# The end of a one-core transformer block: last term's weights gated on GpSimd, last row in two halves

## The chip, the cores and the metric

The kernel runs on one core of a Trainium2 chip. The time is device microseconds of one execution, as the median over several; the profile is of one further execution, recorded by the hardware profiler. Engines are named as in the profile: PE does matmuls (PEld is its weight load), DVE is the vector engine, ACT the scalar engine, POOL is GpSimd, SP issues most DMAs.

## The reference, cut to what matters

One layer of a hybrid block over x of 1024 rows by 1024 columns, all in float32: an adaptive RMSNorm, a projection, a state-space mixer and chunked attention side by side, an output projection, then a feed-forward part and a final norm. Only the last lines matter here:

```python
    x = x + g_m * (concat[y_s, y_a] @ w_out)
    h = rmsnorm(x, norm_ffn_w) * (1 + sc_f) + sh_f
    x = x + g_f * ((silu(g) * val) @ w_down)     # [g, val] = causal_dwconv(h @ w_up)
return rmsnorm(x, final_norm_w)
```

`g_f`, the gate, is one factor for each of the 1024 columns, the same for all rows. Gating the product `(...) @ w_down` is therefore the same as gating the columns of `w_down` ahead of the product.

## The kernel before, in words

A float32 matmul is made of three matmuls in a faster format: each operand is split into a high part (a rounding copy, on ACT, L93) and a low part (source minus high part, on DVE, L94), and `mm3` (L83 to L86) adds high·high, high·low and low·high. In the final product the operand that streams (`a`, a slice of `w_down`) has 512 columns, and the one that is loaded as weights (`b`, a slice of the hidden state) 128 rows of x at a time. `wsplit` (L1231) puts both parts into one of five ring buffers named `w`.

The down projection is not computed as one product but, by a Strassen-like scheme, as seven products of halves, in the order P1, Q5, Q6, Q7, Q4, P3, P2. Each runs over 11 slices `k` of 128 hidden channels, taken in six pairs `m` (the sixth has one slice), and over four row blocks `st`: 11·4·3 = 132 matmuls of 512 columns. The slices come from DRAM through 14 slots `s0` to `s13` (`load`, L1473). For P3 the weights are the sum of two slices (`add`, L1566, on DVE); P2 takes `w_down` as it is.

The result has eight row blocks of 128 and two column halves. The right halves (columns 512 to 1023) and rows 4 to 7 are complete before the end. For each of them DVE multiplies by the gate `gf` (L1616), loads and adds the residual (L1619, L1620), ACT sums the squares (L1630), and for right halves POOL multiplies by the final norm's weight (L1634). The left half of rows 0 to 3 is the sum of P1 and P2. P1's part (`p1`) is gated and has the residual already; P2 is the last product.

Who runs when is set by a scheduler at build time; each engine then executes its list in order and waits on semaphores. The last part of P2, its pairs 4 and 5 (three slices), is written out by hand (L1712 to L1725) with `InOrder`, which keeps V, A and T in the written order: for each row block nine matmuls, then on DVE the product times the gate (L1719) and the sum with `p1` (L1720), on ACT the squares, on DVE the sum of the two halves' squares, on POOL the power −1/2 (L1130), and then `out_row`: the right half scaled on ACT, the left half on DVE, and two stores on SP. `out_row` of a row stands behind the sums of the next one. In the profile these hand-ordered instructions all carry line L66.

Of the kernel before, what the change touches and what calls it, by code (L numbers as in the profile page):

```python
# [12 lines left out]
AF = mybir.ActivationFunctionType  # L13
ALU = mybir.AluOpType
PSUM = bass.MemoryType.PSUM

P = 128
# [23 lines left out]
KH = NF // 2  # L41
# [31 lines left out]
def tile_block(ctx: ExitStack, tc: tile.TileContext, x, ccol, pk, w_ada, w_first, w_ft, w_z,  # L73
               w_out, w_up, w_down, bias, fnw, out, dbg=None):
    nc = tc.nc
    V, A, T = (InOrder(tc, e) for e in (nc.vector, nc.scalar, nc.tensor))
    G = nc.gpsimd
# [5 lines left out]
    def mm3(ps, lh, ll, rh, rl, start, stop, more=False):  # L83
        T.matmul(ps, lh, rh, start=start, stop=False, skip_group_check=more)  # L84
        T.matmul(ps, lh, rl, start=False, stop=False, skip_group_check=more)  # L85
        T.matmul(ps, ll, rh, start=False, stop=stop, skip_group_check=more)  # L86
# [28 lines left out]
    def stat(n=1):  # L115
        if stc[0] + n > 64:
            stc[0] = 0
        a = st1[:, stc[0]:stc[0] + n]
        stc[0] += n
        return a  # L120
# [18 lines left out]
    def raw_tile(n=1024):  # L139
        rawc[0] += 1  # L140
        return raws[:, rawc[0] % 2, 0:n]
# [227 lines left out]
    for j in range(2):  # L369
        k = slice(4 * j, 4 * j + 4)  # L370
# [48 lines left out]
    for hh in range(2):  # L419
# [12 lines left out]
        tail = range(split_at, KT)  # L432
        for kt in range(KT):
            if hh == 0:
# [7 lines left out]
                t = raw_tile(768)  # L442
# [21 lines left out]
            if hh == 0:  # L464
                for st in range(4, NT):
# [3 lines left out]
                    if XM[st - 4] == kt:  # L469
                        e = A if st < 6 else V  # L470
# [173 lines left out]
    def gemm_part(p, which, hhs):  # L644
        if which == 0:
            new_pair(p)
        if which == 2 and hhs == H1:
            wh, wl = held.pop(p)
        elif p == 2 and which < 2:
            with tc.issue_after(wpin[0].ins), tc.issue_after(wpin[1].ins):  # L650
                wh, wl = wu_pair(w_ft[8 + 3 * (p - 2) + which], A, V)
        else:
            wh, wl = wu_pair(w_ft[8 + 3 * (p - 2) + which], A, G)
        if which == 2 and hhs == H0:
            held[p] = wh, wl
        outs = {hh: psv.tile([P, 512], F32, tag="acc", bufs=1, name="acc") for hh in hhs}
        gemm_ft(wh, wl, outs, GPIN.get((p, which, hhs), {}), hhs)
        for hh in hhs:
            tmp = tps = None
            if which == 2:  # L660
                tmp, tps = p_tile()[:, 0:512], tp_tile()
            evac_qkv(p, which, hh, outs[hh], tmp, tps)
# [15 lines left out]
    part = lambda *a: (lambda: gemm_part(*a))  # L678
# [78 lines left out]
    halves = [slice(0, 512), slice(512, 1024)]  # L757
# [241 lines left out]
    def ssd_y(c, xdt, xdd, cb, ms_):  # L999
        cs = slice(c * P, (c + 1) * P)  # L1000
        prev, cur = state[c % 2], state[(c + 1) % 2]
        ydp = ssd_tile("ydp")
        for h in range(8):
            pe(T.matmul, ydp[:, h * 64:h * 64 + 64], ms_[h // 4][:, h % 4, :],
               xdt[:, h * 64:h * 64 + 64], start=True, stop=True)
        y = sp.tile([P, 512], F32, tag="yy", bufs=2, name="yy")
        with tc.issue_after(powd[0]) if c == 1 else ExitStack():
            i = G.tensor_tensor(h8(y), h8(xs[:, c, :]), hb("p", c), ALU.mult)
        if c < 2:
            z_fine(c, i.ins)  # L1010
        t = sp.tile([P, 512], F32, tag="yt", bufs=2, name="yt")
        if c > 0:
            yop = ssd_tile("yop")
            for g in range(2):
                pe(T.matmul, yop[:, g * 256:g * 256 + 256], ct_[g][:, cs], prev[:, g * 256:g * 256 + 256],
                   start=True, stop=True)
        if c < NT - 1:
            stp = ssd_tile("stp")
            for g in range(2):
                pe(T.matmul, stp[:, g * 256:g * 256 + 256], cb[:, 2 + g, :],  # L1020
                   xdd[:, g * 256:g * 256 + 256], start=True, stop=True)
            if c > 0:
                with tc.issue_after(powd[0]) if c == 1 else ExitStack():
                    G.tensor_tensor(h8(cur), h8(prev), hb("cd", c), ALU.mult)
                V.tensor_tensor(cur, stp, cur, ALU.add)
            else:
                A.activation(cur, stp, AF.Copy)
        V.tensor_tensor(y, ydp, y, ALU.add)
        if c > 0:
            V.tensor_tensor(h8(t), h8(yop), hb("ea", c), ALU.mult)  # L1030
            V.tensor_tensor(y, y, t, ALU.add)
        return y, t
# [17 lines left out]
    NM = (KH + 1) // 2  # L1050

    def kn(m):
        return min(2, KH - 2 * m)

    gd = {}
    for m in range(NM):
        for n, names in (("x", ("b11",)), ("y", ("t1", "t3")), ("z", ("t2", "t4", "b21", "b22"))):
            t = gd[n, m] = dram.tile([kn(m), P, len(names), 512], F32, name=f"g{n}{m}")
# [68 lines left out]
    def rstd2(m):  # L1127
        ms, r = stat(), stat()
        V.scalar_tensor_tensor(ms, m[0], EPS, m[1], op0=ALU.add, op1=ALU.add)
        G.tensor_tensor(r, ms, mhalf[:, 0:1], ALU.pow)  # L1130
        return r
# [4 lines left out]
    for c in range(NT):  # L1136
        if c == 1:
            ssd_turn(*turn)
        y, t = ssd_y(c, *pre)
# [10 lines left out]
        n, k = ((0, slice(0, 3)), (2, slice(0, 4)), (3, slice(0, 3)))[c] if c < 3 else (c + 1, slice(0, 3))  # L1150
# [196 lines left out]
    for sts in ((0, 1), (2, 3)):  # L1347
        h_raw(sts)
        c = slice(sts[0] * P, sts[-1] * P + P)
# [23 lines left out]
    row = lambda u, o: (lambda: u.sums((o,)))  # L1373
# [7 lines left out]
    c = slice(384, 512)  # L1381
# [43 lines left out]
    lo = [u.prep("Q7", "Q4", True) for u in units]  # L1425
# [79 lines left out]
    def take(n, m):  # L1505
        t = res.pop((n, m))
        for slot in [k for k in busy if busy[k] == (n, m)]:
            del busy[slot]
        return t
# [38 lines left out]
    R4 = range(4)  # L1548
    sub = ALU.subtract

    gf, fnr = (t[:, 0:2, :].rearrange("p a b -> p (a b)") for t in (ya, xs))
# [12 lines left out]
    def add(o, a, b):  # L1564
        with tc.issue_after(los[max(0, len(los) - 3)]):
            V.tensor_tensor(o, a, b, ALU.add)  # L1566
        return o
# [3 lines left out]
    def operands(p, m):  # L1571
        a11, a21, a22 = (res[n, m] for n in ("a11", "a21", "a22"))
        b = take(BN[p], m)
        if p == "Q5":
            add(a11, a11, a21)
            add(a21, a21, a22)
        elif p == "Q6":
            add(a21, a11, a22)
        elif p in ("P3", "P2"):
            a = take("a12" + p, m)  # L1580
            if p == "P3":
                add(a, a, a21)
            return a, b
        return dict(P1=a11, Q5=a21, Q6=a21, Q7=a11, Q4=a22)[p], b

# [3 lines left out]
        pump()  # L1589
        return ab  # L1590

    def step(ps, ab, k, sts):
        a, b = (t[:, :, k % 2, :] for t in ab)
        for st in sts:
            c = slice(st * P, (st + 1) * P)
            mm3(ps[st], b[:, 0, c], b[:, 1, c], a[:, 0, :], a[:, 1, :], k == 0, k == KH - 1)

    def product(p, ps, ready=(), tail=False, between=None):
        last = []
        for m in RM:  # L1600
            ab = ready[m] if m < len(ready) else split_pair(p, m)
            if between:
                between(m)
            for k in range(2 * m, 2 * m + kn(m)):
                if tail and m >= NM - 2:
                    last.append((ab, k))
                else:
                    step(ps, ab, k, R4)
        return last

    def xt_():
# [10 lines left out]
    jc, sq = [0], {}  # L1622

    def junk_():
        jc[0] += 1
        return junk[jc[0] % 6]

    def square(row, dh, src):
        sq[row, dh] = stat()
        A.activation(junk_(), src, AF.Square, scale=1.0 / 32.0, accum_out=sq[row, dh])  # L1630

    def right_half(row, src):
        square(row, 1, src)
        G.tensor_tensor(src, src, fnr[:, halves[1]], ALU.mult)  # L1634

    def out_row(row, lo, hi, r):
        t = buf(("a11_0", "a11_1", "a11_2", "a11_3", "a22_0", "a22_1", "a22_2", "a22_3")[row])
        A.activation(t[:, halves[1]], hi, AF.Copy, scale=r)
        V.scalar_tensor_tensor(t[:, halves[0]], lo, r, fnr[:, halves[0]], op0=ALU.mult, op1=ALU.mult)
        for dh in (1, 0):  # L1640
            nc.sync.dma_start(out[row * P:(row + 1) * P, halves[dh]], t[:, halves[dh]])

    def final(row, lo, hi):
        square(row, 0, lo)
# [2 lines left out]
    def rows(ts):  # L1647
        return [t[:, 512 * j:512 * j + 512] for t in ts for j in range(2)]
# [22 lines left out]
    p1, u2 = (rows([c_tile(n), c_tile(n)]) for n in "gv")  # L1671
# [14 lines left out]
    u3 = rows([buf("u30"), buf("u31")])  # L1686
# [18 lines left out]
    W = banks("d")  # L1705
    last = product("P2", W, tail=True)
# [5 lines left out]
    for e in (T, V, A):  # L1712
        e.on, e.last = True, None
    ready = []
    for st in R4:
        for ab, k in last:
            step(W, ab, k, (st,))
        e = junk_()
        V.tensor_tensor(e, W[st], gf[:, halves[0]], ALU.mult)  # L1719
        V.tensor_tensor(p1[st], p1[st], e, ALU.add)  # L1720
        square(st, 0, p1[st])
        if ready:
            out_row(*ready.pop())
        ready.append((st, p1[st], u3[st], rstd2((sq[st, 0], sq[st, 1]))))
    out_row(*ready.pop())  # L1725
    T.on = V.on = A.on = False
    es_s.close()
    es_ht.close()
# [52 lines left out]
```

## Time and profile before

| What | Value |
|---|---|
| time, median of 3 runs (lowest, highest) | 1173.13 us (1171.16, 1173.28) |
| the profiled execution's span | 1173.1 us |
| mean granted PE clock | 0.995 of full speed |
| PE busy | 1152.5 us, 98% of the span |
| DVE busy | 908.3 us, 77% |
| ACT busy | 586.0 us, 50% |
| POOL busy | 155.5 us, 13% |

No other time of the profiled execution is on the page than its span, which lies 0.03 us under the median. A row of the timeline gives the start in us, the duration, the engine, the line, the operation, the tiles written and read, the shape, and in brackets how long the engine stood idle before and what ended it. A row with x3 merges three neighbours of one kind; its duration is from the first start to the last end.

### The profile page before, as it was taken

To read this page: it belongs to the slowest core of one execution; us is meant where nothing else is said; L and a number is where in the kernel's file an instruction comes from. 1 tells how busy PE (TensorE), PEld (TensorE's weight loads), DVE (VectorE), ACT (ScalarE), POOL (GpSimd) and SP (SyncE) were. 2 spreads that over 40 slices of the span, in tenths; PEclk is the share of its full clock that TensorE was granted. 3 is DMA by queue.
4 is the path that set the end of the run, shared out by engine and by line. 5 is a ranking of instruction groups with operands and counts; after the bars stand their busy time and mean duration, and the time that the engine had idled before them with its cause. 6 is when DMAs were issued, how large, how long until landed. Compare 5 with 4: busy or idle time off the path is not lost.

```text
span 1173.1 us, 15823 instructions
## 1 busy us (share of the span) xinstructions
PE 1152.5 (98%) x5851; PEld 977.1 (83%) x5851; DVE 908.3 (77%) x1352; ACT 586.0 (50%) x978; POOL 155.5 (13%) x179
## 2 busy tenths in 40 slices
PE   8999999999999999999999999999999999999997
PEld 7888888788889988887788888888888888888885
DVE  6846555588896779569999988898888869666986
ACT  5636555664335576586453444334533445433454
POOL 2103232340000256100000000000000000000621
PEclk8999999999999999999999999999999999999999
DMA  8835333155578622241223322332233378633544
GB/s 308 305 93 147 79 84 81 39 180 173 183 247 284 245 82 81 77 140 36 99 108 135 115 80 92 118 130 77 90 108 117 117 273 300 252 117 126 162 135 153
DMA packets 63741, 169.15 MB, mean 144 GB/s; under 512 B 6880, under 2 KB 7344, under 8 KB 62256
## 3 DMA queue, kind: packets, MB, share of 16 engines
q1 hardware_dynamic: 56320, 143.11, 37.0%
q10 hardware_dynamic: 7344, 25.04, 5.4%
q8 instruction: 46, 0.75, 0.3%
q14 instruction: 31, 0.25, 0.1%
HBM read 125.87 MB, written 32.81 MB: 135 GB/s over the span
## 4 chain that ended last, share of the span: by engine, by line
PE 86%; DVE 8%; ACT 3%; issue 2%; POOL 1%; DMA 0%; SPq 0%; POOLq 0%; ACTq 0%; DVEq 0%
PE wops L885 6%; PE dn L86 5%; PE dn L85 5%; PE dn L84 5%; PE uY L86 5%; PE uY L84 5%; PE uY L85 5%; PE uX L86 3%; PE uZ L84 3%; PE uZ L86 3%; PE uZ L85 3%; PE uX L84 3%; PE uX L85 3%; PE s L84 3%; PE s L86 3%; PE s L85 3%
## 5 line engine op out<-in xcount | busy, mean ns | idle before, releaser
L84 PE MATMUL dn<-w 128*128 128x512 f32 x296 | 107.4, 389 | 0.0
L85 PE MATMUL dn<-w 128*128 128x512 f32 x296 | 107.4, 389 | 0.0
L86 PE MATMUL dn<-w 128*128 128x512 f32 x296 | 99.9, 390 | 0.1
L84 PE MATMUL uY<-tH,w 128*128 128x512 f32 x248 | 96.5, 389 | 0.0
L86 PE MATMUL uY<-tH,w 128*128 128x512 f32 x248 | 96.5, 389 | 0.0
L85 PE MATMUL uY<-tL,w 128*128 128x512 f32 x248 | 96.5, 389 | 0.0
L1634 POOL TENSOR_TENSOR ya<-ya,xs 128x512 f32<-128x512 f32 x4 | 18.2, 4588 | 551.0 <-ACT xs L1630 551.0
L93 ACT ACTIVATE w<-ya 128x1024 fp32r<-128x1024 f32 (+1 forms) x41 | 39.1, 954 | 85.2 <-PE uY L86 75.2
L885 PE MATMUL wops<-hH,yhl 128*128 128x512 f32 x224 | 73.0, 397 | 1.2 <-DVE yhl L94 1.2
L86 PEld LDWEIGHTS dn<-w 128*128 128x128 f32 x296 | 55.4, 188 | 12.1 <-DVE w L94 0.8
L85 PEld LDWEIGHTS dn<-w 128*128 128x128 f32 x296 | 55.6, 188 | 11.6
L84 PEld LDWEIGHTS dn<-w 128*128 128x128 f32 x296 | 55.6, 188 | 11.6
L557 POOL TENSOR_SCALAR p<-p,st 128x640 f32<-128x640 f32 (+4 forms) x64 | 44.2, 699 | 114.8 <-DVE st L556 111.0
L93 ACT ACTIVATE w<-xs 128x1024 fp32r<-128x1024 f32 (+1 forms) x41 | 39.1, 955 | 37.0 <-PE uY L86 31.0
L551 DVE CUSTOM_DVE_ANT_0 p<-s,bias 128x640 f32<-128x640 f32 (+4 forms) x58 | 38.0, 673 | 23.1 <-PE tp L586 9.6
L94 DVE TENSOR_TENSOR pt<-tp,pt 128x512 fp32r<-128x512 f32 (+2 forms) x72 | 41.6, 595 | 17.3 <-ACT pt L93 17.0
L86 PEld LDWEIGHTS uY<-tH,w 128*128 128x128 f32 x248 | 46.6, 188 | 9.7
L85 PEld LDWEIGHTS uY<-tL,w 128*128 128x128 f32 x248 | 46.6, 188 | 9.7
L84 PEld LDWEIGHTS uY<-tH,w 128*128 128x128 f32 x248 | 46.6, 188 | 9.6
L1308 DVE SCALAR_TENSOR_TENSOR a<-cv,pkt,a 128x1023 f32<-128x1023 f32 (+1 forms) x40 | 50.9, 1275 | 0.1
L84 PE MATMUL s<-hH,wh 128*128 128x512 f32 x128 | 50.6, 395 | 0.1
L885 PEld LDWEIGHTS wops<-hH,yhl 128*128 128x128 f32 x224 | 41.9, 188 | 10.2 <-DVE yhl L94 2.0
(507 smaller groups left out, 3397.2 us busy)
## 6 DMA issues: line engine op xcount, KB each, us to landing
xs<-in_w_ada_dram SPq DMA_DIRECT2D x20, 512.0 KB, 4.6
gz<-a ACTq DMA_DIRECT2D x10, 1024.0 KB, 5.1
ya<-in_w_up_dram SPq DMA_DIRECT2D x11, 768.0 KB, 4.4
xs<-in_w_up_dram SPq DMA_DIRECT2D x11, 768.0 KB, 4.2
adat<-in_w_ada_dram SPq DMA_DIRECT2D x16, 512.0 KB, 7.1
raws<-in_w_ft_dram SPq DMA_DIRECT2D x15, 512.0 KB, 3.9
qk<-qk SPq DMA_DIRECT2D x56, 128.0 KB, 2.3
wos<-in_w_ada_dram SPq DMA_DIRECT2D x12, 512.0 KB, 4.6
```

The costliest lines, as they stand in the source:

```text
L84: T.matmul(ps, lh, rh, start=start, stop=False, skip_group_check=more)
L85: T.matmul(ps, lh, rl, start=False, stop=False, skip_group_check=more)
L86: T.matmul(ps, ll, rh, start=False, stop=stop, skip_group_check=more)
L93: i = A.activation(hi, src, AF.Copy) if ehi is A else ehi.tensor_copy(hi, src)
L94: return i, elo.tensor_tensor(lo, src, f32(hi), ALU.subtract)
L551: V.tensor_tensor_reduce(out=dst, in0=src, in1=bsl, scale=-1.0, scalar=3e38, op0=ALU.add, op1=ALU.min, accum_out=nm)
L557: last_g.append(G.tensor_scalar(pv_, pv_, rr, 1.0, op0=ALU.mult, op1=ALU.mult).ins)
L885: i = op(*a, **k)
L1308: V.scalar_tensor_tensor(a[:, j:S], c[:, 0:S - j], w[2 - j], a[:, j:S], op0=ALU.mult, op1=ALU.add)
L1634: G.tensor_tensor(src, src, fnr[:, halves[1]], ALU.mult)
```

## The change

Three edits. First, in `operands`, P2's slice of `w_down` is multiplied in place by the left half of the gate on POOL, between its load and its split: five multiplies of 128x1024 and one of 128x512. In the last stage DVE's multiply by the gate goes away; DVE adds the product straight from PSUM to `p1`. Second, the last row block's nine tail matmuls of 512 columns become two sets of nine with 256 columns; after each set DVE adds that half and ACT sums its squares, and a further small DVE addition joins the first half's sum of squares to the right half's. Third, of the last row's two stores the right half is issued on ACT's queue; the left stays on SP.

```diff
             if p == "P3":
                 add(a, a, a21)
+            else:
+                G.tensor_tensor(a, a, gf[:, 0:512].unsqueeze(1).to_broadcast([P, kn(m), 512]), ALU.mult)
             return a, b
...
+    def half_step(ps, ab, k, c, o):
+        a, b = (t[:, :, k % 2, :] for t in ab)
+        for l, r in ((0, 0), (0, 1), (1, 0)):
+            T.matmul(ps[:, o], b[:, l, c], a[:, r, o], start=False, stop=True, skip_group_check=True)
...
         for dh in (1, 0):
-            nc.sync.dma_start(out[row * P:(row + 1) * P, halves[dh]], t[:, halves[dh]])
+            q = nc.scalar if last and dh else nc.sync
+            q.dma_start(out[row * P:(row + 1) * P, halves[dh]], t[:, halves[dh]])
...
-    for st in R4:
+    for st in range(3):
         for ab, k in last:
             step(W, ab, k, (st,))
-        e = junk_()
-        V.tensor_tensor(e, W[st], gf[:, halves[0]], ALU.mult)
-        V.tensor_tensor(p1[st], p1[st], e, ALU.add)
+        V.tensor_tensor(p1[st], p1[st], W[st], ALU.add)
         square(st, 0, p1[st])
...
+    part = sq[3, 1]
+    for n, c in enumerate((slice(0, 256), slice(256, 512))):
+        for ab, k in last:
+            half_step(W[3], ab, k, slice(3 * P, 4 * P), c)
+        V.tensor_tensor(p1[3][:, c], p1[3][:, c], W[3][:, c], ALU.add)
+        square(3, 0, p1[3][:, c])
+        if n == 0:
+            both = stat()
+            V.tensor_tensor(both, part, sq[3, 0], ALU.add)
     out_row(*ready.pop())
+    out_row(3, p1[3], u3[3], rstd2((both, sq[3, 0])), True)
```

Where the scheduler puts the six multiplies on POOL: in this piece of the difference (− before, + after), `ya` are rows 4 to 7 and `dnH_8170` rows 0 to 3 of the right halves; L1584 are the new multiplies, in the order of the pairs 0 to 5, and their tiles are load slots.

```order
-L1634 TENSOR_TENSOR ya<-ya,xs 128x512 x4
-L1634 TENSOR_TENSOR dnH_8170<-dnH_8170,xs 128x512 x4
+L1642 TENSOR_TENSOR ya<-ya,xs 128x512 x3
+L1584 TENSOR_TENSOR dns_8087<-dns_8087,ya 128x1024
+L1642 TENSOR_TENSOR ya<-ya,xs 128x512
+L1584 TENSOR_TENSOR dnH_8090<-dnH_8090,ya 128x1024 x2
+L1584 TENSOR_TENSOR dnL_8166<-dnL_8166,ya 128x1024
+L1642 TENSOR_TENSOR dnH_8170<-dnH_8170,xs 128x512 x2
+L1584 TENSOR_TENSOR dnL_8166<-dnL_8166,ya 128x1024
+L1642 TENSOR_TENSOR dnH_8170<-dnH_8170,xs 128x512
+L1584 TENSOR_TENSOR dna_8278<-dna_8278,ya 128x512
+L1642 TENSOR_TENSOR dnH_8170<-dnH_8170,xs 128x512
```

The first multiply comes ahead of row 7's, the second to fourth behind it. On DVE the rows of these stages keep their order, as these of the third product before the end show (after; `dnH_8170<-dnH_8170,dn` reads a PSUM bank, `w` rows are low parts):

```order
L1566 TENSOR_TENSOR dnL_8166<-dnL_8166,dnL_8096 128x1024
L1708 TENSOR_TENSOR dnH_8170<-dnH_8170,dn 128x512
L94 TENSOR_TENSOR w<-dnH_8090,w 128x1024
L1708 TENSOR_TENSOR dnH_8170<-dnH_8170,dn 128x512 x3
L94 TENSOR_TENSOR w<-dnH_8090,w 128x1024
L1566 TENSOR_TENSOR dna_8278<-dna_8278,dnb21h 128x1024
L1624 TENSOR_TENSOR dnH_8170<-dnH_8170,ya 128x512
```

Apart from line numbers (L1699 became L1708, L1616 became L1624), these rows stand so before too. On PE the end reads, after:

```order
L66 MATMUL dn<-w 128x512 [waits DVE_49] x2
L66 MATMUL dn<-w 128x512 x18
L66 MATMUL dn<-w 128x256 x9
L66 MATMUL dn<-w 128x256 [waits DVE_49]
L66 MATMUL dn<-w 128x256 x8
```

Before, 27 matmuls of 512 columns stood there without a wait. Now the second half's first matmul waits for DVE: its event is the addition of the first half, which reads the same PSUM bank. On DVE the last row's part reads, after (`cg<-cg,dn` are the two half additions, the 128x1 rows the sums of squares, `dnb11l` the scaled left halves of rows 2 and 3):

```order
L66 SCALAR_TENSOR_TENSOR st_72<-st_72 128x1 [waits Activation_49]
L66 TENSOR_TENSOR cg<-cg,dn 128x256 [waits PE_49]
L66 TENSOR_TENSOR st_72<-st_72 128x1 [waits Activation_49]
L66 TENSOR_TENSOR cg<-cg,dn 128x256 [waits PE_49]
L66 SCALAR_TENSOR_TENSOR dnb11l<-cg,st_72,xs 128x512 [waits Pool_49]
L66 SCALAR_TENSOR_TENSOR st_72<-st_72 128x1 [waits Activation_49]
L66 SCALAR_TENSOR_TENSOR dnb11l<-cg,st_72,xs 128x512 [waits Pool_49]
```

The first half's addition stands behind row 2's sum of squares, and row 2's scaling behind the second half's addition.

More of the change, by code (lines that the diff above doesn't have):

```diff
@@ L1590, in split_pair, with step @@
         return ab
-    def step(ps, ab, k, sts):
+    def step(ps, ab, k, sts, halved=False):
         a, b = (t[:, :, k % 2, :] for t in ab)
@@ L1595, in step @@
             c = slice(st * P, (st + 1) * P)
-            mm3(ps[st], b[:, 0, c], b[:, 1, c], a[:, 0, :], a[:, 1, :], k == 0, k == KH - 1)
+            mm3(ps[st], b[:, 0, c], b[:, 1, c], a[:, 0, :], a[:, 1, :], k == 0,
+                k == KH - 1 or halved and k == 2 * NM - 5 and st == 3)
+    def half_step(ps, ab, k, c, o):
+        a, b = (t[:, :, k % 2, :] for t in ab)
+        for l, r in ((0, 0), (0, 1), (1, 0)):
+            T.matmul(ps[:, o], b[:, l, c], a[:, r, o], start=False, stop=True, skip_group_check=True)
     def product(p, ps, ready=(), tail=False, between=None):
@@ L1607, in product @@
                 else:
-                    step(ps, ab, k, R4)
+                    step(ps, ab, k, R4, tail)
         return last
@@ L1629, in square @@
         sq[row, dh] = stat()
-        A.activation(junk_(), src, AF.Square, scale=1.0 / 32.0, accum_out=sq[row, dh])
+        A.activation(junk_()[:, 0:src.shape[-1]], src, AF.Square, scale=1.0 / 32.0, accum_out=sq[row, dh])
     def right_half(row, src):
@@ L1634, in right_half, with out_row @@
         G.tensor_tensor(src, src, fnr[:, halves[1]], ALU.mult)
-    def out_row(row, lo, hi, r):
+    def out_row(row, lo, hi, r, last=False):
         t = buf(("a11_0", "a11_1", "a11_2", "a11_3", "a22_0", "a22_1", "a22_2", "a22_3")[row])
```

## The prediction

> **What bounds the kernel now.** I read the page's busy times first, then the chain of waits from 1100 us on.
>
> ```profile
> PE 1152.5 (98%) x5851; PEld 977.1 (83%) x5851; DVE 908.3 (77%) x1352; ACT 586.0 (50%) x978; POOL 155.5 (13%) x179
> ```
>
> ```profile
> 1106.90 1.64 DVE w L94
> 1108.54 1.79 DVE dnH L1699 x3
> 1110.33 1.13 DVE w L94
> ...
> 1116.14 1.15 DVE w L94
> 1117.33 1.21 PE dn L86 x4
> ...
> 1156.66 2.05 PE dn L66 x9
> 1160.18 0.73 ACT xs L66 x2
> ```
>
> PE is the bound: what makes it wait is lost, as it has no later gap in which to catch up. There are two places near the end where DVE sets the pace of PE. One is the third product (P3), 1106 to 1117 us: the low parts made by DVE at L94 come just in time, and PE's weight loads wait for two of them:
>
> ```profile
> 1111.52 0.76 PEld L86 LDWEIGHTS dn<-w 128*128 128x128 f32 x4 [0.30 <-DVE w L94]
> 1117.33 0.77 PEld L86 LDWEIGHTS dn<-w 128*128 128x128 f32 x4 [0.49 <-DVE w L94]
> ```
>
> The other is the tail from 1158.7 us, where the chain goes through DVE, ACT and POOL. The change takes work out of the tail and puts work on POOL before it. So the question is whether POOL's work reaches DVE in the first place.
>
> The timeline answers that. DVE in the tight stretch, then three of POOL's present multiplies (128x512, two inputs in SBUF):
>
> ```profile
> 1102.84 1.23 DVE L94 TENSOR_TENSOR w<-dnL,w 128x1024 fp32r<-128x1024 f32 x1 [2.31 <-ACT w L93]
> 1103.98 2.31 DVE L1566 TENSOR_TENSOR dnL<-dnL,dnL 128x1024 f32<-128x1024 f32 x1
> 1106.22 0.68 DVE L1699 TENSOR_TENSOR dnH<-dnH,dn 128x512 f32<-128x512 f32 x1
> 1106.82 1.72 DVE L94 TENSOR_TENSOR w<-dnH,w 128x1024 fp32r<-128x1024 f32 x1
> 1108.46 1.87 DVE L1699 TENSOR_TENSOR dnH<-dnH,dn 128x512 f32<-128x512 f32 x3
> 1110.25 1.21 DVE L94 TENSOR_TENSOR w<-dnH,w 128x1024 fp32r<-128x1024 f32 x1
> 1111.39 1.21 DVE L1566 TENSOR_TENSOR dna<-dna,dnb21h 128x1024 f32<-128x1024 f32 x1
> ```
>
> ```profile
> 1089.21 12.48 POOL L1634 TENSOR_TENSOR ya<-ya,xs 128x512 f32<-128x512 f32 x1 [550.99 <-ACT xs L1630]
> ...
> 1102.91 2.31 POOL L1634 TENSOR_TENSOR ya<-ya,xs 128x512 f32<-128x512 f32 x1
> 1105.18 2.27 POOL L1634 TENSOR_TENSOR ya<-ya,xs 128x512 f32<-128x512 f32 x1
> ```
>
> A 128x1024 DVE operation takes 1.21 us, and two of these take 2.31 and 1.72. Both overlap POOL: L1566 ends 1.1 us after POOL's multiply ends at 1105.22, and L94 ends 1.1 us after the next, at 1107.45. DVE stood still until POOL was through. The reverse holds as well: POOL's 12.48 us multiply ended at 1101.69, 1.2 us after DVE, busy without a pause until then, fell idle (2.31 us before 1102.84). Only L1699, which reads one input from PSUM, kept its 0.68 us beside POOL. So in these rows two-input operations of DVE and POOL exclude each other for their whole length.
>
> **The change part by part.** The sum is made on the profiled execution's span of 1173.1 us, which is the median of the runs, so nothing is added between them.
>
> *The multiplies on POOL.* Their nearest row is POOL's other two-input operation of 128x1024, at 2.39 us; the 128x512 ones take 1.29 us where nothing holds them.
>
> ```profile
> L94 POOL TENSOR_TENSOR wl<-raws,wh 128x1024 fp32r<-128x1024 f32 x7 | 16.7, 2394 | 24.4 <-ACT wh L93 23.4 <-PE acc L86 1.0
> 1129.73 1.29 POOL L1634 TENSOR_TENSOR dnH<-dnH,xs 128x512 f32<-128x512 f32 x1 [1.99 <-ACT xs L1630]
> ```
>
> Five at 2.39 and one at 1.29 are 13.2 us. POOL is idle enough for that, and if DVE never met them they would cost nothing. I follow POOL's new order from 1105.2 us, when row 6's multiply ends. The first gate multiply waits for L1566, starts at about 1106.25 beside L1699, and ends at 1108.6: L94 is held until then instead of 1107.4, and ends at 1109.7 instead of 1108.5. PE needs that part four matmuls before the load at 1111.52, from about 1110.6; no loss. Row 7's multiply, now behind it, waits for L94, then runs beside the three L1699 (1109.6 to 1111.4) until 1110.9. The second gate multiply is next in the queue, and its slice has been there since 1105.3:
>
> ```profile
> dnH<-in_w_down_dram SPq DMA_DIRECT2D x1, 512.0 KB, 4.7
> ```
>
> (that load was issued at 1100.57). So it starts at 1110.9, half a microsecond before DVE asks for its next L94, the one for which PE waits at 1111.52. It holds until 1113.2; L94 ends at 1114.4 instead of 1111.46. PE loses **2.9 us** there, and nothing covers it. Ends: 0 if DVE is first each time, 1.1 if only the first multiply holds it, and not over the 2.9, as the multiply's length is known. Behind the held L94 all of DVE's list moves by 2.9, and so do ACT and the loads that wait for it, which keeps the later distances to PE as they are.
>
> The rest of POOL's list, three multiplies of 2.39, one of 1.29 and four right halves of 1.29, is 13.6 us. The third multiply's slice is loaded only after the held L94s, lands at about 1113, and finds DVE in its run up to 1122.5. I let it wait as the 12.48 us row did, for the gap there, which it just fills:
>
> ```profile
> 1124.77 0.69 DVE L1620 TENSOR_TENSOR dnH<-dnH,xs 128x512 f32<-128x512 f32 x1 [2.29 <-DMA xs<-x1d]
> 1125.38 2.91 DVE L94 TENSOR_TENSOR w<-dna,w 128x1024 fp32r<-128x1024 f32 x2
> ...
> 1130.20 1.37 DVE L94 TENSOR_TENSOR w<-dna,w 128x512 fp32r<-128x512 f32 x1 [1.31 <-ACT w L93]
> ```
>
> ```profile
> 1132.47 0.39 PE L86 MATMUL dn<-w 128*128 128x512 f32 x1
> ```
>
> The fourth multiply and two right halves (2.39 + 2·1.29 = 5.0) then meet DVE between 1124.8 and 1131.6, less the gap of 1.31: 3.7 us of delay, where the rows hold 1.8 already (1.37 for 128x512, which takes 0.69; 2.91 for one of 1024 columns and one of 512, 1.8 elsewhere). That is 1.9 more, against 0.9 of slack (the split ends at 1131.57, PE uses it at 1132.47): 1.0 lost. In P2 the last two multiplies and two right halves are left (6.3 us), of which 2.7 lie beside four additions from PSUM (0.68 each, as L1699); slack is 2.0 at its second pair
>
> ```profile
> 1138.77 1.21 DVE L94 TENSOR_TENSOR w<-dnL,w 128x1024 fp32r<-128x1024 f32 x1
> ```
>
> ```profile
> 1141.99 1.07 PE L86 MATMUL dn<-w 128*128 128x512 f32 x4
> ```
>
> and grows after it, so of the 3.6 I take 0.9 as lost. Together **1.9 us**. Ends: 0, if all of it falls into gaps, and 7.3, if all of the 13.6 less the gaps (2.29 + 1.31 + 2.7) reaches PE. I take 1.9 because the rows with slack are the ones it meets.
>
> *The tail's multiply and the halves.*
>
> ```profile
> 1156.49 8.32 PE L66 MATMUL dn<-w 128*128 128x512 f32 x36
> 1158.73 0.69 DVE L66 TENSOR_TENSOR xs<-dn,ya 128x512 f32<-128x512 f32 x1 [0.64 <-PE dn L66]
> ...
> 1165.69 0.68 DVE L66 TENSOR_TENSOR xs<-dn,ya 128x512 f32<-128x512 f32 x1
> 1166.41 0.69 DVE L66 TENSOR_TENSOR cg<-cg,xs 128x512 f32<-128x512 f32 x1
> 1167.94 0.16 DVE L66 SCALAR_TENSOR_TENSOR st<-st 128x1 f32<-128x1 f32 x1 [0.18 <-ACT xs L66]
> ```
>
> 36 matmuls in 8.32 us are 0.2266 apart, a row of nine 2.04. DVE takes the first row at 1158.73, 0.43 after its ninth matmul started, and the last at 1165.69, although its ninth started at 1164.43: DVE lags 0.83. (The first three rows' multiplies are covered by PE's next nine matmuls but for this lag.) Without the multiply (0.72) the lag goes too, so an unhalved last row would have its sum of squares 1.55 earlier than 1167.94. The halves take part of that back, by the new wait. A 256-column matmul stands 0.12 apart:
>
> ```profile
> 40.37 0.28 PE L66 MATMUL vps<-wsl,hH 128*128 128x256 f32 x1
> 40.49 0.28 PE L66 MATMUL vps<-wsh,hH 128*128 128x256 f32 x1
> ```
>
> First half: ninth start at 1162.61 + 8·0.12 = 1163.57, ready 1164.00. But row 2's sum of squares is ahead on DVE: its addition at 1162.82, plus the 1.53 from addition to sum (1166.41 to 1167.94), is 1164.35. The half addition runs from 1164.4 to 1164.8 (0.42 by the 128x256 row below); only then may PE go on. Second half: ninth start 1164.9 + 0.96, ready 1166.3, added by 1166.7; squares of a half are 0.2 shorter, but row 2's scaling (0.75) stands before the sum, which comes at about 1167.3. Gain **0.6**. Ends: a loss of 1.1, if 256 columns cost PE as much as 512; a gain of 1.8, if the wait fell on an older event. The small joining addition hides behind the second half's matmuls.
>
> ```profile
> L94 DVE TENSOR_TENSOR pt<-tp,pt 128x256 fp32r<-128x256 f32 x16 | 6.7, 416 | 4.4 <-ACT pt L93 4.4
> ```
>
> *Two queues.* SP issues the last row's stores one behind the other; with ACT's queue the second needs no turn. Gain **0.4**, at least 0 if ACT's issue holds something up.
>
> ```profile
> 1169.51 0.33 SPq L1641 DMA_DIRECT2D out_dram<-dnb11l  x1
> 1169.94 0.38 SPq L1641 DMA_DIRECT2D out_dram<-dnb11l  x1
> ```
>
> Sum: 1173.1 + 2.9 + 1.9 − 0.6 − 0.4 = **1176.9 us**.
>
> **The rivals.** *First come, first served.* In my sum the third multiply waits through DVE's run. The row at 1102.91 speaks otherwise: POOL asked during an L94 and was served before L1566. Then the third multiply enters at 1114.4, in front of the second place where PE has no slack (1117.33), and costs its 2.39 in full: 1179.3, and 1181 if the fourth does likewise. The 12.48 us row speaks against it. [...] Chance 0.25.
>
> *POOL always yields* (the other side). If DVE keeps its run against POOL each time, POOL works only in gaps and beside PSUM operations: 0.6 at 1106.3, 1.8 at 1108.5, 2.3 at 1122.5, 1.3 at 1128.9 and 2.7 in P2, together 8.7, and the first three gate multiplies with row 7's need 8.5. They would be in time, DVE would lose nothing, and only the tail's 1.0 would be left: 1172.1, or 1170.9 where the halves also avoid their wait. It is decided at 1110.9: if the second multiply comes 0.5 us later, DVE is there first. Against it: the 1.72 row, where POOL kept DVE waiting in just that way. Chance 0.25 for this and what lies between it and 1175.4.
>
> **How the numbers follow.** My forecast (1175.5 to 1179) has 0.5, first come 0.25, yielding 0.25. A difference under 0.2%, 2.3 us, can't be told from none. Faster needs yielding and free halves: 0.1. Within 0.2% is the rest of that rival with the low end of the forecast: 0.2. Slower: 0.7. The range goes from 1172.1 (the tail alone) to 1181.5 (first come, with the fourth), with about 0.1 outside on each side.
>
> **What would show it.** In the changed profile: a weight load of PE near 1111.5 that waits about 3 us for DVE's L94, with that L94 or one beside it 3 us long; POOL's L1584 rows of 2.4 us or more; the end of P2's matmuls 4 to 5.5 us later; in the tail a DVE period that follows PE, a gap in PE of 1.0 to 1.3 us between the two halves, and the last sum of squares 0.6 us closer to PE's tail start. It is wrong if P3 runs through without a wait longer than now, or if the POOL rows stretch over many microseconds while DVE keeps its 1.21.

## The result and the profile after

| What | before | after |
|---|---|---|
| time, median of 5 runs (lowest, highest) | 1172.91 us (1171.16, 1173.28) | 1181.37 us (1180.97, 1184.96) |
| ratio, 95% interval | | 1.0079 [1.0067, 1.0091] |
| span of the profiled execution | 1173.1 us | 1179.6 us |
| POOL's first final-norm multiply to PE's tail start | 67.28 us | 76.50 us |
| PE's tail start to the last sum of squares | 11.45 us | 10.85 us |
| last sum of squares to the end | 5.16 us | 5.36 us |

The kernel is 8.5 us slower. I had forecast 3.8 us slower: the sign was right, the size less than half. The changed kernel's profiled execution took 1181.37 us, 1.8 us more than its span. If the same lies around before's span, that execution took about 1174.9 us, 2 us above its median, and these 2 us lie ahead of the change: POOL's first final-norm multiply starts at 1089.21 us there and at 1086.93 after. About 1.5 us of them are PE's clock at the start: over the first 30 us the granted clock averages 0.89 before and 0.94 after. So stretches are compared from POOL's row on. They give 9.22 − 0.60 + 0.20 = 8.8 us (to the hundredth the spans are 1173.11 and 1179.65 us).

PE's share is the same as before, as the page's first line shows. POOL is busy for 20 us more, of which the six multiplies unhindered would be 13.2 us; a row counts as busy while its operation stands still, too (the fourth gate multiply's row is 6.54 us long, the second's 2.36):

```profile
PE 1154.2 (98%) x5860; PEld 977.7 (83%) x5860; DVE 915.9 (78%) x1350; ACT 586.1 (50%) x980; POOL 175.8 (15%) x185
```

The loss is in PE's idle time. The groups of PE's instructions from 1095 us on; the last column is the idle time before them and what ended it:

```profile
L85 PE MATMUL dn<-w 128*128 128x512 f32 x88 | 31.7, 399 | 0.2 <-DVE w L94 0.2
L84 PE MATMUL dn<-w 128*128 128x512 f32 x84 | 30.5, 397 | 1.2 <-ACT w L93 1.2
L86 PE MATMUL dn<-w 128*128 128x512 f32 x88 | 29.9, 400 | 5.3 <-DVE w L94 5.3
L66 PE MATMUL dn<-w 128*128 128x512 f32 (+1 forms) x45 | 8.7, 349 | 1.1 <-DVE cg L66 1.1
```

PE waits for operand parts (5.3, 1.2 and 0.2 us) and once, 1.1 us, for the first half of the last row. Where the waits for parts stand, by the timeline:

```profile
1111.99 1.20 PE L86 MATMUL dn<-w 128*128 128x512 f32 x4 [2.63 <-DVE w L94]
1117.06 1.20 PE L85 MATMUL dn<-w 128*128 128x512 f32 x4 [0.24 <-DVE w L94]
1120.00 1.20 PE L86 MATMUL dn<-w 128*128 128x512 f32 x4 [1.74 <-DVE w L94]
1136.02 0.50 PE L84 MATMUL dn<-w 128*128 128x512 f32 x1 [1.22 <-ACT w L93]
1137.66 0.50 PE L86 MATMUL dn<-w 128*128 128x512 f32 x1 [0.91 <-DVE w L94]
```

All five are in P3, the last two at its last split. The wait for ACT there goes back to DVE as well. On ACT that split stands behind the squares of row 3's right half, and these wait for DVE's addition of the residual, which comes late and takes 2.88 us instead of 0.68 beside POOL's fifth gate multiply (1131.30 to 1134.14):

```profile
1131.81 2.88 DVE L1628 TENSOR_TENSOR dnH<-dnH,xs 128x512 f32<-128x512 f32 x1
```

ACT takes the squares at 1134.72, the split at 1135.35, and PE goes on at 1136.02. A wait costs PE about 0.27 us more than its bracket says: a matmul's row lasts 0.39 us while the next one normally starts after 0.227, and the matmul behind the waiting one comes 0.11 late. So the five cost 2.90, 0.51, 2.01, 1.49 and 1.18, in all 8.1 us; before loses 0.5 at the same places. Now POOL's rows in that stretch, and DVE's:

```profile
1102.90 3.38 POOL L1584 TENSOR_TENSOR dns<-dns,ya 128x1024 f32<-128x1024 f32 x1
1106.24 2.29 POOL L1642 TENSOR_TENSOR ya<-ya,xs 128x512 f32<-128x512 f32 x1
1108.49 2.36 POOL L1584 TENSOR_TENSOR dnH<-dnH,ya 128x1024 f32<-128x1024 f32 x1
1111.13 3.06 POOL L1584 TENSOR_TENSOR dnH<-dnH,ya 128x1024 f32<-128x1024 f32 x1 [0.28 <-DMA dnH<-in_w_down_dram]
1120.87 6.54 POOL L1584 TENSOR_TENSOR dnL<-dnL,ya 128x1024 f32<-128x1024 f32 x1 [6.69 <-issue]
```

```profile
1104.54 2.82 DVE L94 TENSOR_TENSOR w<-dnH,w 128x1024 fp32r<-128x1024 f32 x1
1107.28 1.87 DVE L1708 TENSOR_TENSOR dnH<-dnH,dn 128x512 f32<-128x512 f32 x3
1109.07 2.86 DVE L94 TENSOR_TENSOR w<-dnH,w 128x1024 fp32r<-128x1024 f32 x1
1111.86 3.41 DVE L1566 TENSOR_TENSOR dna<-dna,dnb21h 128x1024 f32<-128x1024 f32 x1
...
1121.60 1.28 DVE L1628 TENSOR_TENSOR dnH<-dnH,xs 128x512 f32<-128x512 f32 x2
...
1123.94 1.22 DVE L94 TENSOR_TENSOR w<-dna,w 128x1024 fp32r<-128x1024 f32 x1
1127.09 0.87 DVE L1628 TENSOR_TENSOR dnH<-dnH,xs 128x512 f32<-128x512 f32 x1 [1.94 <-DMA xs<-x1d]
```

The first three gate multiplies each hold a DVE operation of 1.21 us: L94 takes 2.82 and 2.86 us, L1566 3.41, and each ends 1.1 us after the POOL multiply beside it, about its own length of 1.21. L1708, with one input in PSUM, keeps 0.62 us apiece between them. The fourth multiply is the one that waits: it starts at 1120.87, lets at least four DVE operations pass at full speed, and ends at 1127.41, 2.25 us after DVE fell idle at 1125.16.

One loss is no wait. The windows view of two stretches (length, busy time of PE, PEld, DVE, ACT, POOL, then the granted PE clock, DMA's share and GB/s):

```profile
1106.00:1112.00 6.00, 3.37 (x16) 2.46 (x14) 6.00 (x6) 2.01 (x2) 5.72 (x4) 1.00 0.29 87
1136.00:1142.00 6.00, 5.08 (x14) 3.73 (x15) 6.00 (x5) 2.92 (x4) 2.75 (x2) 0.72 0.12 40
```

A mean of 0.72 over 6 us is a clock of one half for 3.4 us: from 1138.5 to 1141.5 us it reads 0.50. Behind the last wait seven or eight matmuls stand 0.427 us apart instead of 0.227: 1.6 us.

In the tail DVE now follows PE; the second half's matmuls wait for the first half's addition, which stands behind row 2's sum of squares (PE's rows, then DVE's):

```profile
1163.43 7.38 PE L66 MATMUL dn<-w 128*128 128x512 f32 x36
1171.86 0.39 PE L66 MATMUL dn<-w 128*128 128x256 f32 x1 [1.05 <-DVE cg L66]
```

```profile
1171.32 0.16 DVE L66 SCALAR_TENSOR_TENSOR st<-st 128x1 f32<-128x1 f32 x1 [0.19 <-ACT xs L66]
1171.39 0.41 DVE L66 TENSOR_TENSOR cg<-cg,dn 128x256 f32<-128x256 f32 x1
...
1174.29 0.16 DVE L66 SCALAR_TENSOR_TENSOR st<-st 128x1 f32<-128x1 f32 x1
```

From 1163.43 to 1174.29 are 10.85 us. The last two stores are issued by SP and by ACT, both at about 1175.9, and the execution ends at 1179.6. ACT's:

```profile
1175.86 0.37 ACTq L1650 DMA_DIRECT2D out_dram<-dnb11l  x1
```

### The profile page after: what moved, and what is told of

The parts are those of the page before. It is cut to its first block, busy times and chain, and to the rows that moved or that the text cites. A ratio compares the mean times of both kernels' runs of the same rounds, so it can differ in the third digit from the quotient of the medians.

```text
span 1179.6 us, 15848 instructions
## 1 busy us (share of the span) xinstructions
PE 1154.2 (98%) x5860; PEld 977.7 (83%) x5860; DVE 915.9 (78%) x1350; ACT 586.1 (50%) x980; POOL 175.8 (15%) x185
## 5 line engine op out<-in xcount | busy, mean ns | idle before, releaser
L94 DVE TENSOR_TENSOR pt<-tp,pt 128x512 fp32r<-128x512 f32 (+2 forms) x72 | 41.7, 596 | 17.3 <-ACT pt L93 16.9
L86 PE MATMUL s<-hH,wl 128*128 128x512 f32 x128 | 50.3, 393 | 0.0
```

Of the source, the lines that this page charges most:

```text
L94: return i, elo.tensor_tensor(lo, src, f32(hi), ALU.subtract)
```

## The experiments

Three theories. **A**: POOL's multiplies shut DVE's two-input operations out for their whole length, and PE waits for a late DVE. **B**, a rival: the new dependency costs, since a split must wait for the gated slice. **C**, a rival: the halves and the second queue cost the time. The kernel before was timed again beside each group of experiments. Its medians are 1172.89 us beside the first four, 1172.72 beside the next four and 1172.49 beside the last three.

### The first edit alone (gate_only)

```diff
+            else:
+                G.tensor_tensor(a, a, gf[...], ALU.mult)
...
-        e = junk_()
-        V.tensor_tensor(e, W[st], gf[:, halves[0]], ALU.mult)
-        V.tensor_tensor(p1[st], p1[st], e, ALU.add)
+        V.tensor_tensor(p1[st], p1[st], W[st], ALU.add)
```

> Only the first edit: P2's slices gated on POOL, DVE adds the product straight to p1; the last row stays whole and all stores stay on SP. Theory A (two-input operations of POOL and DVE exclude each other, and DVE comes late for PE): the gate's cost of about 9 us stays, less about 1.5 us that DVE's tail gains without the multiply: 7 to 8 us slower than before, with the same PE waits of 2 to 3 us at L86 and a stretch of half clock behind them. Theory C (the halves and the second queue cost the time): 1 to 2 us faster than before. This run does not tell exclusion from theory B (the split has to wait for the gated slice): B expects the same 7 to 8 us.

1179.57 us, ratio 1.0059 [1.0047, 1.0071]: 6.7 us slower by the medians. C falls as the main cause: of the 8.5 us, about 1.8 are left to the halves and the queue. The last sum of squares stands 9.93 us behind PE's tail start, 1.52 less than before. So the tail gains what the removed multiply and its lag were worth, and the halves, with 10.85, cost 0.9 us of it. PE's waits and one window of its clock:

```profile
1112.83 1.24 PE L86 MATMUL dn<-w 128*128 128x512 f32 x4 [2.63 <-DVE w L94]
1120.83 1.20 PE L86 MATMUL dn<-w 128*128 128x512 f32 x4 [0.63 <-DVE w L94]
1136.94 0.50 PE L84 MATMUL dn<-w 128*128 128x512 f32 x1 [1.28 <-ACT w L93]
1138.58 0.50 PE L86 MATMUL dn<-w 128*128 128x512 f32 x1 [0.91 <-DVE w L94]
```

```profile
1112.00:1118.00 6.00, 5.17 (x16) 4.09 (x17) 6.00 (x5) 0.00 (x0) 2.99 (x1) 0.72 0.26 87
```

Here the half clock came behind the first wait. PE then used its parts up more slowly, the wait of 0.24 us near 1117 is gone, and the one near 1120 us shrank from 1.74 to 0.63: as DVE was late anyway, 1.35 us of the slow clock's 1.6 came back in shorter waits.

### The same multiplies, written aside (gate_aside)

```diff
+            else:
+                j = buf("a22_4", kn(m) * 512).rearrange("p (k c) -> p k c", c=512)
+                G.tensor_tensor(j, a, gf[...], ALU.mult)
```

The split reads `a` as it was loaded and DVE still multiplies in the tail; nobody reads `j`.

> The kernel before with six more multiplies on POOL of the same size, from the same slices, in the same places of POOL's order, but written to a buffer that nobody reads, so that no split waits for them; the tail is that of before. Theory A (exclusion): the full cost of the gate, about 9 us slower than before (8 to 10), L94 rows of 2.8 us, PE waits at L86 of 2 to 3 us. Theory B (the split waits for the gated slice): within 1 us of before, L94 rows of 1.2 to 1.8 us as before. Theory C (halves and queue): within 1 us of before.

1180.88 us, ratio 1.0070 [1.0056, 1.0083]: 8.0 us slower, although no split waits for a multiply. B falls, A holds. POOL's third multiply, DVE and PE's first wait read as in the changed kernel (the profiled execution, at 1183.78 us, is the longest of the six):

```profile
1111.95 2.99 POOL L1585 TENSOR_TENSOR dnb21l<-dnH,ya 128x1024 f32<-128x1024 f32 x1 [0.32 <-DMA dnH<-in_w_down_dram]
```

```profile
1105.32 2.82 DVE L94 TENSOR_TENSOR w<-dnH,w 128x1024 fp32r<-128x1024 f32 x1
...
1112.63 3.39 DVE L1566 TENSOR_TENSOR dna<-dna,dnb21h 128x1024 f32<-128x1024 f32 x1
```

```profile
1112.76 1.69 PE L86 MATMUL dn<-w 128*128 128x512 f32 x4 [2.62 <-DVE w L94]
```

### The second and third edit alone (halves_queue)

The changed kernel without its multiply on POOL; rows 0 to 2 keep DVE's multiply and addition of before, and the halves get their own:

```diff
-            else:
-                G.tensor_tensor(a, a, gf[...], ALU.mult)
...
-        V.tensor_tensor(p1[3][:, c], p1[3][:, c], W[3][:, c], ALU.add)
+        e = junk_()[:, 0:256]
+        V.tensor_tensor(e, W[3][:, c], gf[:, c], ALU.mult)
+        V.tensor_tensor(p1[3][:, c], p1[3][:, c], e, ALU.add)
```

> The second and third edit without the first: last row in two halves of 256 columns, last right half stored by ACT's queue, DVE still multiplies by the gate in the tail. Theories A and B: no cost before the tail; in the tail the second half waits for the first half's multiply, which stands behind DVE's lag, so the last sum of squares comes 1 to 2 us later: 1 to 2 us slower than before. Theory C: 5 us slower or more.

1174.66 us, ratio 1.0013 [1.0005, 1.0021]: 1.8 us slower. As the main cause, C is out. Without the gate the halves lose outright, since the first half's multiply stands behind DVE's lag, and PE waits 2.29 us:

```profile
1164.76 1.33 PE L66 MATMUL dn<-w 128*128 128x256 f32 x9 [2.29 <-DVE xs L66]
```

### The second queue alone (queue_only)

```diff
+            q = nc.scalar if row == 3 and dh else nc.sync
+            q.dma_start(out[row * P:(row + 1) * P, halves[dh]], t[:, halves[dh]])
```

> The kernel before, with the last row's right half stored by ACT's queue. My prediction's term: 0.4 us faster. Rival (the two transfers share what they need and the later one lands no earlier, as the changed kernel's end looks): within 0.2 us of before, the last landing 3.5 to 3.8 us after the last operation of DVE.

1172.69 us, ratio 0.9998 [0.9990, 1.0007]: no difference. In the traces the stretch from the last sum of squares to the end is 5.34 us here and 5.36 in the run above and in the changed kernel, against 5.16 to 5.19 in the ten kernels that store by SP alone. If anything the queue costs 0.2 us.

### The multiplies on DVE (gate_dve)

```diff
+            else:
+                with tc.issue_after(los[max(0, len(los) - 3)]):
+                    V.tensor_tensor(a, a, gf[...], ALU.mult)
```

> The first edit alone, but with the six multiplies on DVE instead of POOL; their place in DVE's order is the scheduler's (the first behind P3's fourth addition of slices, the last before P2's last two pairs). Theory A (exclusion): on DVE a multiply of 128x1024 costs DVE 1.21 us instead of the 2.4 us for which POOL's shuts it out: 6.7 us in all, against 2.3 + 1.3 + 2.5 us of gaps that DVE had behind 1122 us; PE loses 0 to 2 us, the tail gains 1.5: between 1.5 us faster and 0.5 us slower than before. Theory B (what costs is that the split waits for a gated slice): 5 us slower or more, as with POOL.

1172.93 us, ratio 1.0004 [0.9996, 1.0013]: no difference, where the same multiplies on POOL cost 6.7 us. B expected 5 us or more and falls a second time. The place is another one too: the first of these multiplies stands at 1117.92 us, behind P3's tight stretch. That alone does not explain the difference, as multiplies at a later place on POOL (gate_late0, below) cost 7.5 us. DVE's groups for the multiplies (busy, mean ns):

```profile
L1585 DVE TENSOR_TENSOR dnH<-dnH,ya 128x1024 f32<-128x1024 f32 x2 | 3.5, 1764 | 0.0
...
L1585 DVE TENSOR_TENSOR dns<-dns,ya 128x1024 f32<-128x1024 f32 x1 | 1.2, 1209 | 0.0
```

One of the first two met POOL (2.31 us). They take 1.21 us where POOL leaves DVE alone, half of what POOL's own version shuts DVE out for. The gain of the tail was not reached: its last sum of squares stands 10.85 us behind PE's tail start, not 9.9.

### Shorter multiplies on POOL (gate_pieces)

```diff
+                for j in range(kn(m)):
+                    G.tensor_tensor(a[:, j, :], a[:, j, :], gf[:, 0:512], ALU.mult)
```

> The first edit alone, with each multiply of 128x1024 on POOL cut into two of 128x512 (1.29 us each). Theory A, length (DVE is shut out for one POOL operation at a time and then has its turn): the PE wait of 2.6 us near the third product's end shrinks to 1.3 to 1.6 us, the time is 3 to 5.5 us slower than before, clearly under the 6.9 of the uncut multiplies. Theory A, sum (only the total of POOL's work beside DVE counts): 6 to 8 us slower, as uncut.

1178.86 us, ratio 1.0060 [1.0048, 1.0072]: 6.1 us slower. Each wait is another one, the sum is nearly the same:

```profile
1109.75 1.19 PE L86 MATMUL dn<-w 128*128 128x512 f32 x4 [0.46 <-DVE w L94]
1115.91 1.20 PE L85 MATMUL dn<-w 128*128 128x512 f32 x4 [1.33 <-DVE w L94]
1119.95 2.07 PE L86 MATMUL dn<-w 128*128 128x512 f32 x4 [2.84 <-DVE w L94]
```

With the 0.13 and 0.94 us at P3's last split that is 5.7 us, against 5.45 in gate_only. The wait near 1112 us did shrink (0.46 us, at 1109.75), but its pieces came back later. POOL's four pieces in a row:

```profile
1108.56 8.44 POOL L1585 TENSOR_TENSOR dnH<-dnH,ya 128x512 f32<-128x512 f32 x4
```

That is 2.1 us each beside DVE, of 1.29 us of work: with a turn for DVE after each piece, DVE gets through sooner at one place and comes later at the next.

### Later multiplies on POOL (gate_late0)

```diff
+                with tc.issue_after(rh[4]):
+                    G.tensor_tensor(a, a, gf[...], ALU.mult)
```

`rh` collects POOL's multiplies by the final norm's weight; `rh[4]` is row 0's.

> The first edit alone, with the multiplies held back in POOL's order until row 0's right half is done (about 1123 us), so that none meets P3's tight stretch. Theory A, sum: the PE waits of 2.6, 0.2 and 1.7 us in P3 are gone, but three multiplies more stand between 1123 and 1145 us, where DVE has 3 to 4 us of gaps, so PE waits there for 5 us or more: 4 to 7 us slower than before. Rival (it is only the tight place that costs): 0.5 to 2.5 us slower (the 2.1 us of waits and up to 1.6 of half clock there, less 1.5 in the tail).

1180.18 us, ratio 1.0064 [1.0051, 1.0077]: 7.5 us slower, 0.5 above the 4 to 7 expected. P3's tight stretch is as before, and the loss stands behind it:

```profile
1128.09 1.20 PE L86 MATMUL dn<-w 128*128 128x512 f32 x4 [1.42 <-DVE w L94]
1134.94 0.80 PE L84 MATMUL dn<-w 128*128 128x512 f32 x1 [2.93 <-ACT w L93]
1137.66 0.80 PE L86 MATMUL dn<-w 128*128 128x512 f32 x1 [1.50 <-DVE w L94]
```

5.85 us of waits, against 5.45 and 5.7. So in these three runs neither the place nor the length of the multiplies changes much; what they have in common is the sum of POOL's work beside a DVE list that has no room for it.

### The first three multiplies alone, aside (aside_first3)

The edit of gate_aside with `elif m < 3:` in place of `else:`.

> As the run with six multiplies written aside, but only the first three of them. Theory A: the PE waits of 2.6 and 0.2 to 0.7 us and the one at 1120 us (0.6 to 1.7), and a stretch of half clock behind one of them in some executions; nothing is lost in P2: 3.5 to 5.5 us slower than before, with a PE that runs through from 1121 us on. Rival (each multiply costs the same wherever it stands): half of the 8.0 us, with waits in P2 as well.

1176.55 us, ratio 1.0037 [1.0024, 1.0050]: 3.8 us slower. PE waits at the same three places as in the changed kernel, and nowhere later:

```profile
1111.99 1.20 PE L86 MATMUL dn<-w 128*128 128x512 f32 x4 [2.63 <-DVE w L94]
1117.06 1.19 PE L85 MATMUL dn<-w 128*128 128x512 f32 x4 [0.23 <-DVE w L94]
1120.00 1.79 PE L86 MATMUL dn<-w 128*128 128x512 f32 x4 [1.75 <-DVE w L94]
```

```profile
1118.00:1124.00 6.00, 4.25 (x13) 3.14 (x12) 6.00 (x9) 1.34 (x4) 0.88 (x1) 0.72 0.65 198
```

The waits are those of the changed kernel to 0.01 us, but here the half clock came behind the third, where in the changed kernel the clock stayed full. This profiled execution, at 1179.09 us, is the longest of the four.

### Towards a faster kernel (gate_dve3, gate_dve2, tail_order)

gate_dve lost its tail at two rows, 0.14 and 0.25 us of PE waiting for P2's last split, which stood behind the scaling of other rows. So the scaling of rows 6 and 7 (gate_dve3), or 5 to 7 (gate_dve2), was put behind it:

```diff
-        final(4 + st, u2[st], q5[st])
+        with tc.issue_after(los[-1]) if st >= 2 else ExitStack():
+            final(4 + st, u2[st], q5[st])
```

In gate_dve2 `st >= 1` stands there.

> The multiplies on DVE as in the run before, and the scaling of rows 6 and 7 put behind P2's last split in DVE's and ACT's order, because there PE's tail waited 0.14 + 0.25 us (and stepped 0.3 to 0.6 us apart) for that split. Theory A: the tail's 0.9 us come back, so that the last sum of squares stands 9.9 to 10.0 us behind PE's tail start instead of 10.85; before the tail 1.0 to 1.3 us stay lost: 0.2 to 1.0 us faster than the kernel before. If PE's smaller steps before the tail grow instead, no faster.

1172.58 us, ratio 1.0001 [0.9992, 1.0009]; last sum 10.20 us behind PE's tail start.

> As that run, with row 5's scaling behind the last split too. Theory A: the split comes earlier still, but three scalings (2.2 us) then stand between the sums of the tail's rows 0 and 1, which DVE gets back by row 3 only in part: 0 to 0.7 us faster than the kernel before, at most 0.3 us from the run with two.

1172.07 us, ratio 0.9998 [0.9990, 1.0007]; last sum 9.90 us behind. The tail's gain of 1.55 us is there in full, but PE loses 1.24 us before it, mostly at four places of 0.1 to 0.4 us where DVE's list is now tight. What is left, 0.3 us from POOL's first multiply to the end, can't be measured.

```diff
         V.tensor_tensor(e, W[st], gf[:, halves[0]], ALU.mult)
+        if st:
+            ready.append((st - 1, ..., rstd2((sq[st - 1, 0], sq[st - 1, 1]))))
         V.tensor_tensor(p1[st], p1[st], e, ALU.add)
         square(st, 0, p1[st])
         if ready:
             out_row(*ready.pop())
-        ready.append((st, ..., rstd2((sq[st, 0], sq[st, 1]))))
+    ready.append((3, ..., rstd2((sq[3, 0], sq[3, 1]))))
```

> The kernel before, with DVE's order in the tail changed alone: the next row's multiply by the gate stands ahead of the previous row's sum of squares, so that DVE does not wait 0.2 to 0.8 us for ACT with work at hand. By my rows the last multiply would start 0.3 to 0.5 us after PE instead of 0.83: 0.3 us faster, at the edge of what can be measured. Rival (DVE's scaling, 0.74 us a row, sets its pace whatever the order): within 0.1 us.

1172.81 us, ratio 1.0004 [0.9995, 1.0012]: no gain; the last sum stands 11.87 us behind PE's tail start, 0.4 later than before. My expectation left out POOL's power: before, the next row's multiply and addition hide it; with the sum of squares put off, the scaling waits 0.44 us for it.

```profile
1162.48 0.75 DVE L66 SCALAR_TENSOR_TENSOR dnb11h<-cg,st,xs 128x512 f32<-128x512 f32 x1 [0.44 <-POOL st L1130]
```

No kernel tried beats the kernel before by an amount that can be measured.

## Why the prediction was right in sign and wrong in size

| Step | forecast, us | measured in the trace, us |
|---|---|---|
| second multiply holds L94, PE waits | +2.9 | +2.9 |
| third multiply | 0 | +2.5, of which before has 0.4 |
| the rest of POOL's list | +1.9 | +2.7 |
| half clock behind the waits | none | +1.6 |
| tail's multiply and halves | −0.6 | −0.6 |
| two queues | −0.4 | +0.20 |

Less the 0.5 that before loses at the same places, the column on the right gives 8.8.

**Right.** The exclusion, read from two stretched rows of the kernel before, and its price at the place named: a weight load near 1111.5 us that waits about 3 us, where it waited 0.30 before:

```profile
1111.98 0.76 PEld L86 LDWEIGHTS dn<-w 128*128 128x128 f32 x4 [3.06 <-DVE w L94]
```

The runs without a split that waits (gate_aside) and without POOL's multiplies (gate_dve) showed the two sides of it. Right too were the tail's numbers: the gap of 1.0 to 1.3 us between the halves (1.05), and the last sum of squares 0.6 us closer to PE's tail start.

**The step that failed** is "I let it wait as the 12.48 us row did, for the gap there, which it just fills". The third multiply did not wait: it asked at 1111.13 during an L94 and held the next DVE operation, L1566, for 3.41 us. That is my first rival, and its price of 2.39 was near the 2.2 us measured (2.52 less 0.36 before). The fourth multiply then did what I had expected of the third: 6.54 us, through DVE's run, into the gap. So the rival is right at one place and my reading at the next. I had taken one row (12.48 us) as the rule, against another row (1102.91) that I quoted as its opposite.

What decides the turn was not tested, but the brackets of POOL's rows sort it. Before, in the changed kernel and in gate_pieces, gate_late0, aside_first3, gate_dve and gate_dve2, from POOL's first final-norm multiply on, and in gate_only and gate_aside between 1102 and 1130 us, the POOL multiplies that let further DVE operations pass are just those before which POOL had stood idle for 6.5 us or more: 551 us (the 12.48 us row), 13.0, 8.9, and 6.5 to 6.7 (the fourth gate multiply, three times). Each that came within 3.2 us of POOL's last work was held up by no more than the DVE operation under way. The row at 1102.91 came without idle time and the third multiply after 0.28 us, so by this the two rows of before did not contradict each other. The turn mattered less than I thought: uncut, cut or later, the multiplies cost 6.1 to 7.5 us on POOL.

**The rest** was too small by 0.8. Of its 1.9 us, 1.0 stood at P3's last split, where both waits of together 2.7 are, and 0.9 in P2, which lost nothing.

**Missing** from the sum was the clock, at 1.6 us. I priced every wait as its own length.

**The queues** were priced at the turn that the second store no longer needs. But the two, both issued at about 1175.9 us, took longer to land, ACT's 2.8 us and SP's 2.6, where before the last two took 2.0 and 2.3; and the end stands 0.2 us further behind the last sum of squares.

## What to carry to other kernels

An idle POOL was no free help for a busy DVE here: a multiply with its inputs in SBUF kept DVE from its own two-input work for 2.4 us, where DVE would have done it in 1.21. Before moving work there, add up the idle gaps that DVE has until PE needs its parts, and compare them with the whole of POOL's work; cutting it up or moving it changed the cost only between 6.1 and 7.5 us. And where two rows of a profile disagree on who goes first, look for what else differs in them, here the idle time in the brackets, and price both for each meeting.

## What the runs showed of the hardware

Behind short waits PE's clock halved for 3.4 us. This came behind a wait of 2.63 us (gate_only), behind 0.23 and 1.75 (aside_first3) and behind 1.22 and 0.91 (the changed kernel), and it stayed away behind the same 2.63 us in the changed kernel. Before, the clock reads 1.00 over 1095 to 1160 us, and from 1100 on PE is idle for 0.06 us in all. In gate_dve, where the longest wait that PE's rows show is 0.25 us, the weight loads between 1105 and 1148 us keep their steps of 0.227. Each of the six kernels with gate multiplies on POOL has a stretch of half clock. The longest are about twice as long: 6.8 us with the later multiplies (means of 0.85 over 1130 to 1136 us and 0.58 over the next 6), and at least 6.5 with the cut ones (the rows here). They begin within waits of 2.93 and 2.84 us:

```profile
1118.00:1124.00 6.00, 4.05 (x10) 3.18 (x11) 6.00 (x6) 0.00 (x0) 3.07 (x2) 0.50 0.44 150
1124.00:1130.00 6.00, 6.00 (x27) 4.94 (x26) 5.91 (x6) 2.92 (x6) 4.77 (x3) 0.96 0.81 270
```

No wait of PE in the stretches shown is longer than 2.93 us. Which waits bring the half clock, and why 2.63 us brought it in one execution and not in another, was not shown.
